# First feed-forward product by seven block products in both layers, the first 256 features plain, and background modulations in three tiles

## The chip, the cores and the metric

One Trainium2 chip, one of its cores. The metric is the device time of one execution in microseconds (us). Engine names in the profile: PE is TensorE's matrix multiply and PEld its weight load, DVE is VectorE, ACT is ScalarE, POOL is GpSimd, SP is SyncE, which issues all the DMAs here.

## What is computed

Two layers of a diffusion backbone run over 256 context tokens and 1024 latent tokens of width 1024. Each layer has a mixer (attention, a gated linear recurrence, a gated MLP) and then a feed-forward part, which alone is changed. `mod` is one vector of six modulations for each stream, computed from a conditioning vector.

```python
mod = silu(cond) @ w_ada[l] + b_ada[l]             # sh1, sc1, g1, sh2, sc2, g2
x   = layernorm(ALPHA * x + g1 * out, ln1_g, ln1_b)
hff = x * (1 + sc2) + sh2
f   = square(relu(hff @ w_ff1[l] + b_ff1[l])) @ w_ff2[l] + b_ff2[l]   # 1024 -> 4096 -> 1024
x   = layernorm(ALPHA * x + g2 * f, ln2_g, ln2_b)
```

All data are float32. Every matrix operand is split into a rounded high part and a low remainder, and each product is the sum of three: high by high, high by low, low by high.

## The kernel before

**Blocks and chunks.** Tokens come in ten blocks of 128: two of the context (group C, 256 columns) and eight of the latents (groups A and B, 512 columns each). The product with `w_ff1` has its output features on the partitions. It runs in 16 chunks (`NCH`) of 256 features, each chunk as two halves `m` of 128.

**The plain form** (`ff1`, layer 0) does for each half and group eight steps of the inner dimension, each with three matmuls (`fm_group`, `mm3`): 96 matmuls of 512 columns and 48 of 256 in a chunk. The weights of a chunk are two pieces, each split by ScalarE (high part, L168) and GpSimd (low part, L172, 128x1024) in `p_emit_split`. ScalarE takes the result out of PSUM with bias and ReLU.

**The seven-product form** (`first_seven`, layer 1, `SL = (1,)`) takes features, inner dimension and latents in two halves each and forms the latents' part of a chunk with seven block products instead of eight. A product has 12 matmuls of 512 columns; the context's columns stay plain, 48 matmuls of 256 columns. It needs sums and differences of weight blocks and of token blocks. For each chunk GpSimd forms four weight blocks (L1560 to L1565) and splits eight (`w1s`, L172), each operation 128x512; `wait` issues these items `WLA` = 4 products ahead. The seven results are combined by VectorE with seven additions that have one operand in PSUM (L1588). The token blocks' sums and differences (`half`, `hitem`) are made once, at the end of `out_proj` and between the products of chunk 0.

**What runs beside it.** `mid_store` writes each chunk's squared result to DRAM; for the first 12 chunks (`2*NQ`) VectorE adds and subtracts four times on 128x640 (L1476 to L1479). `residual` takes one block of the residual stream in each of eleven calls from chunk 2 on: a DMA load, two VectorE operations on 128x1024 (L1422, L1423), a DMA store. In layer 0, from chunk 1 on, a background generator (`ada_bg`) computes seven parts of the modulations, each in two halves of 512 columns. A half loads four slabs `aslab` of 512 KB, accumulates 16 times on VectorE (2 times L484, 14 times L486, 128x512), splits the sum (ScalarE, then GpSimd on 128x1024, `aspl`) and ends with four matmuls `ada` (L495). `tick(us)` advances it by `us * 0.62` (`ABR`) units, and each accumulation costs 0.6 units:

```python
nc.vector.scalar_tensor_tensor(acc[:, s, :], sl, self.sc[:, k, s:s + 1], acc[:, s, :], ALU.mult, ALU.add)
yield 0.6
```

**Order and buffers.** The framework orders each engine's instructions and places the waits; an engine runs its instructions in that order. Tiles of 4 KB a partition come from two pools, `u` (30 tiles) and, during a layer's feed-forward part, `x` (`NX` = 14 tiles), with 8 tiles `m` beside it. PSUM has 8 banks, shared by all products of the stage.

Of the kernel before, what the change touches and what calls it, by code (L numbers as in the profile page):

```python
# [15 lines left out]
P = 128  # L16
# [5 lines left out]
NCH = 16  # L22
# [19 lines left out]
SL = (1,)  # L42
WLA = 4
# [35 lines left out]
class Kern:  # L79
# [149 lines left out]
    def pieces_init(self):  # L229
# [8 lines left out]
        for l in range(DEPTH):  # L238
# [18 lines left out]
    def pal(self, p, stg=False):  # L257
# [5 lines left out]
        if ph == "out" and self.phase == "out" and not stg:  # L263
            return self.mt
        return self.x if ph == self.phase and self.X is not None else self.u
# [203 lines left out]
    def ada_bg(self, l, parts):  # L469
# [3 lines left out]
        for part in parts:  # L473
            for h in range(2):
                acc = self.u([P, 2, 512], s="aacc")
                c0 = part * D + h * 512
                for k in range(8):
                    if k % 2 == 0:
                        sl2 = self.u([P, 2, 512], s="aslab")
# [8 lines left out]
                hi, lo = (self.u([P, 2, 512], F32R, s="aspl") for _ in range(2))  # L488
# [8 lines left out]
                row = self.u([2, 2, 512], s="arow")  # L497
# [49 lines left out]
    def h_from_pair(self, h, t0, xa, xb, ab, lo_pool=None, alloc=None, tmp_act=False):  # L547
# [27 lines left out]

    def h_raw(self, h, t0, xa, xb, ab):

        nc = self.nc
        g = grp(t0)
        if g not in h:  # L580
            h[g] = [self.u([P, 2, 512], s="hr") for _ in range(4)]
        c0 = (t0 - GROUPS[g][0]) * P
        for kp in range(4):
            b = self.ps([P, 2, 256], "hps")
            for kk in range(2):
                k = 2 * kp + kk
                for j, x in enumerate((xa, xb)):
                    nc.tensor.transpose(b[:, kk, j * P:(j + 1) * P], x[:, k * P:(k + 1) * P], self.ident)
            for kk in range(2):
                k = 2 * kp + kk  # L590
                dst = h[g][kp][:, kk, c0:c0 + 256]
                if kk == 0:
                    nc.scalar.activation(dst, b[:, kk, :], AF.Identity, bias=ab[:, 1, 1, k:k + 1], scale=ab[:, 1, 0, k:k + 1])
                else:
                    nc.vector.tensor_scalar(dst, b[:, kk, :], ab[:, 1, 0, k:k + 1], ab[:, 1, 1, k:k + 1], ALU.mult, ALU.add)


    def run(self):
# [8 lines left out]
        for l in range(DEPTH):  # L607
# [12 lines left out]
            h2 = self.out_proj(l, mix)  # L620
            h1 = self.ff(l, h2)
            self.x_close()

    def cst_load(self):
# [32 lines left out]
        self.rows = self.DR.tile([2, D], F32, name="rows")  # L657
        self.ydr = [self.DR.tile([10, P, 4, P], F32, name=f"ydr{l}") for l in range(DEPTH)]
# [664 lines left out]
    def out_proj(self, l, mix):  # L1323
# [31 lines left out]
        for i, t in enumerate(BLOCKS):  # L1355
# [4 lines left out]
            if fs and i == len(BLOCKS) - 2:  # L1360
                fs["half"](0)
            if fs and i == len(BLOCKS) - 1:
                fs["half"](1)
                fs["h"](1)
# [9 lines left out]
            if i >= OW:  # L1374
                if fs:
                    fs["w"](i - OW + 1)
                else:
                    self.p_emit_split(min(self.pidx[(l, "w1", 0, 0)] + i - OW + 1, self.pidx[(l, "w1", 0, 1)] + 1))
            if fs and i == len(BLOCKS) - 1:
                del w  # L1380
# [14 lines left out]
            if len(xq) == 4 or (len(xq) == 3 and xq[0][0] % 2 == 0):  # L1395
                (ta, xa), (tb, xb) = xq.pop(0), xq.pop(0)
                if fs:
                    self.h_raw(h2, ta, xa, xb, ab)
                else:
                    self.h_from_pair(h2, ta, xa, xb, ab, lo_pool=None, tmp_act=True)  # L1400
# [3 lines left out]
        if fs:  # L1404
            fs["h"](2)
            h2["C"] = tuple([al([P, 4, 256], F32R, s="hc") for _ in range(2)] for al in (self.u, self.mt))
        self.late = lambda: self.h_from_pair(h2, ta, xa, xb, ab, lo_pool=None, tmp_act=bool(fs))
        return fs or h2


    def residual(self, l, alloc):
# [4 lines left out]

        def step(i):
            if i == 0:
                st["g"], st["b"] = (self.bc_row(I[k][l:l + 1], "a" + k[-1], ALPHA, alloc=alloc) for k in ("ln1_g", "ln1_b"))
# [16 lines left out]
    def ff1(self, l, c, h2, after):  # L1436
# [6 lines left out]
        for g in "ABC":  # L1443
# [3 lines left out]
            if g == "B":  # L1447
                self.ahead((l, "w1", c, 1), 2, 4, (l, "w1", NCH - 1, 1))
# [571 lines left out]
```

## Time and profile before

| | us |
|---|---|
| median of the runs (3178.54 to 3184.3) | 3180.42 |
| the profiled execution | 3182.43 |
| span from its first to its last instruction | 3180.6 |
| layer 0: first product, 16 chunks (741.40 to 1208.97) | 467.57 |
| layer 1: first product, 16 chunks (2288.62 to 2723.16) | 434.54 |

Times inside the program count from the span's start. The two last lines are read from the first matmul of the stage to the first of the next (tile `mh`, the second feed-forward product). PE is busy 94% of the span, DVE 72%, POOL 48%, ACT 46%.

### The profile page before, as it was taken

The numbers are of one execution on the slowest core, as the hardware profiler recorded it, in microseconds if no ns is written. First come the engines' busy times: TensorE is split into PE (matmuls) and PEld (weight loads), VectorE is DVE, ScalarE is ACT, GpSimd is POOL, SyncE is SP. The second block draws the span as 40 slices with busy tenths as digits, with TensorE's granted clock in tenths as the row PEclk, the third lists the DMA queues.
The fourth block names the chain that finished last, engine by engine and source line by source line (L and its number), as shares of the span: only waits on it lengthen the run. The fifth ranks groups of instructions, "written<-read, shape, count | busy, mean of one in ns | idle before, by whom it ended". The sixth has DMA issues, their size and how long they took to land. (4 is left out here: it accounts for less than half of the span.)

```text
span 3180.6 us, 42699 instructions
## 1 busy us (share of the span) xinstructions
PE 2978.2 (94%) x15816; PEld 2491.2 (78%) x15816; DVE 2281.1 (72%) x4540; ACT 1471.5 (46%) x2268; POOL 1527.9 (48%) x866
## 2 busy tenths in 40 slices
PE   6888999899999999999989889999889999999993
PEld 4677789788888888888777868997778888878883
DVE  8779999765666634878764989996744542487889
ACT  5554578744332324333166438884254444433301
POOL 3222244503322326856743213357565666685776
PEclk9999999999999999999999999999999999999997
DMA  7321000225666654443321110004235453544331
GB/s 226 117 90 56 15 1 8 74 96 191 219 216 228 206 188 148 157 138 112 116 100 34 53 31 1 1 25 138 96 112 174 168 176 137 191 147 145 114 109 66
DMA packets 163392, 367.44 MB, mean 116 GB/s; under 512 B 20792, under 2 KB 58440, under 8 KB 163184
## 3 DMA queue, kind: packets, MB, share of 16 engines
q1 hardware_dynamic: 163184, 364.72, 34.2%
q8 instruction: 124, 2.03, 0.3%
q14 instruction: 84, 0.69, 0.1%
HBM read 261.84 MB, written 102.83 MB: 115 GB/s over the span
## 5 line engine op out<-in xcount | busy, mean ns | idle before, releaser
L172 POOL TENSOR_TENSOR wlo<-stg,whi 128x1024 fp32r<-128x1024 f32 (+2 forms) x116 | 241.5, 2093 | 363.9 <-ACT whi L168 331.9
L176 PE MATMUL ps<-hh,whi 128*128 128x512 f32 (+1 forms) x1040 | 376.7, 363 | 14.3 <-ACT htmp L570 12.4
L177 PE MATMUL ps<-hl,whi 128*128 128x512 f32 (+1 forms) x1040 | 374.4, 360 | 4.5 <-POOL hl L390 2.6
L178 PE MATMUL ps<-hh,wlo 128*128 128x512 f32 (+1 forms) x1040 | 373.5, 359 | 0.0
L176 PE MATMUL ps<-wh,mh 128*128 128x512 f32 x840 | 333.1, 397 | 0.7 <-DVE accy L1770 0.7
L177 PE MATMUL ps<-wl,mh 128*128 128x512 f32 x840 | 331.8, 395 | 0.0
L178 PE MATMUL ps<-wh,ml 128*128 128x512 f32 x840 | 330.7, 394 | 0.0
L172 POOL TENSOR_TENSOR pt<-ptf,pt 128x512 fp32r<-128x512 f32 x128 | 166.6, 1302 | 241.8 <-DVE pt L170 225.8
L172 DVE TENSOR_TENSOR ml<-mf,mh 128x1280 fp32r<-128x1280 f32 x84 | 173.7, 2067 | 118.1 <-ACT mh L168 112.5
L1179 DVE TENSOR_SCALAR_CACHE_REDUCE S<-sc 128x512 f32<-128x512 f32 (+1 forms) x416 | 224.8, 582 | 14.7 <-PE pT L1190 12.5
L168 ACT CAST mh<-mf 128x1280 fp32r<-128x1280 f32 x84 | 106.3, 1265 | 278.8 <-PE ps L177 235.6
L176 PEld LDWEIGHTS ps<-hh,whi 128*128 128x128 f32 x1040 | 196.5, 189 | 47.4 <-ACT htmp L570 12.8
L172 POOL TENSOR_TENSOR wl<-wraw,wh 128x1024 fp32r<-128x1024 f32 x60 | 170.6, 2851 | 117.0 <-ACT wh L168 116.9
L177 PEld LDWEIGHTS ps<-hl,whi 128*128 128x128 f32 x1040 | 196.9, 189 | 37.9 <-POOL hl L390 4.4
L178 PEld LDWEIGHTS ps<-hh,wlo 128*128 128x128 f32 x1040 | 197.6, 190 | 32.8 <-issue 0.2
L1182 ACT ACTIVATE S<-S,anm 128x1280 f32<-128x1280 f32 (+1 forms) x160 | 191.2, 1196 | 38.4 <-DVE anm L1181 36.1
L1190 PE MATMUL pT<-ident,S 128*128 128x128 f32 x1344 | 202.6, 274 | 2.0 <-DVE pt L1199 1.4
L1215 PE MATMUL o<-pt,vt 128*128 128x256 f32 x1024 | 193.1, 304 | 9.7 <-POOL pt L172 7.9
L177 PE MATMUL ps<-slo,w1s 128*128 128x512 f32 x448 | 180.4, 403 | 16.3 <-DVE slo L1504 16.2
L1588 DVE TENSOR_TENSOR f<-ps,f 128x512 f32<-128x512 f32 x112 | 75.8, 688 | 163.2 <-PE ps L178 152.8
L176 PEld LDWEIGHTS ps<-wh,mh 128*128 128x128 f32 x840 | 157.7, 188 | 39.5 <-DVE accy L1770 1.5
L178 PEld LDWEIGHTS ps<-wh,ml 128*128 128x128 f32 x840 | 157.7, 188 | 39.2
(394 smaller groups left out, 8550.0 us busy)
## 6 DMA issues: line engine op xcount, KB each, us to landing
mf<-mc SPq DMA_DIRECT2D x84, 640.0 KB
mc<-s SPq DMA_DIRECT2D x48, 640.0 KB
aslab<-in_w_ada SPq DMA_DIRECT2D x56, 512.0 KB
stg<-in_w_ff SPq DMA_DIRECT2D x48, 512.0 KB
wraw<-in_w_ff SPq DMA_DIRECT2D x48, 512.0 KB
mc<-f SPq DMA_DIRECT2D x72, 320.0 KB
w1r<-in_w_ff SPq DMA_DIRECT2D x32, 512.0 KB
stg<-in_w_in SPq DMA_DIRECT2D x28, 512.0 KB
```

The source lines that it names most:

```text
L168: nc.scalar.copy(hi, src)
L172: e.tensor_tensor(lo, src, hi.bitcast(F32), ALU.subtract)
L176: mm(out, lh, rh, start=start, stop=False)
L177: mm(out, lh, rl, start=False, stop=False)
L178: mm(out, ll, rh, start=False, stop=stop)
L1179: nc.vector.tensor_scalar(S[:, c0:c0 + n], b[:, :n], 1.0, -3.0e38, ALU.mult, ALU.max, accum_out=u["m"][:, hh, i:i + 1])
L1182: nc.scalar.activation(S[:, :c0], S[:, :c0], AF.Exp, bias=u["nm"][:, hh:hh + 1], accum_out=u["d"]["den"][:, ci % 2, hh:hh + 1])
L1190: nc.tensor.transpose(b[:, c, hh, :], u["S"][hh][:, (2 * j + c) * P:(2 * j + c + 1) * P], self.ident)
L1215: nc.tensor.matmul(o, v, pt[:, hl, c, :], start=j == 0 and c == 0 and hl == 0, stop=j == last and c == 1 and hl == 1)
L1588: add = lambda x, b, y: nc.vector.tensor_tensor(x, b, y, ALU.add)
```

## The change

Both layers take the seven-product form from chunk 1 on (`SL = (0, 1)`, `C0 = 1`); chunk 0 is plain in both. `out_proj` therefore forms the split token blocks with `h_from_pair` in layer 1 too, as layer 0 did, and in both layers also stores the unsplit values to a DRAM tensor `hr`. During chunk 0 they are loaded back (eight tiles of 512 KB) and the sums and differences are formed and split; three of the seven token operands are the plain chunk's own tiles. The context blocks' late transposes move to the middle of chunk 0's group B. `WLA` goes from 4 to 3, and a chunk's weights are loaded at item 6 of the chunk before instead of item 0. `ada_bg` takes its tiles from `x` and lets go of a slab before the next is taken. `tick` is called after each product and each context half. `residual` works on two blocks by half their columns instead of one whole block; the count and size of its operations stay.

```diff
-SL = (1,)
-WLA = 4
+SL = (0, 1)
+C0 = 1
+WLA = 3
@@ pieces_init
-            for c in range(NCH if l not in SL else 0):
+            for c in range(C0 if l in SL else NCH):
@@ ada_bg
-                acc = self.u([P, 2, 512], s="aacc")
+                acc = self.x([P, 2, 512], s="aacc")
-                        sl2 = self.u([P, 2, 512], s="aslab")
+                        sl = sl2 = None
+                        sl2 = self.x([P, 2, 512], s="aslab")
...
+                sl = sl2 = None
+                hi, lo = (self.x([P, 2, 512], F32R, s="aspl") for _ in range(2))
@@ h_from_pair
+            if raw is not None and kp % 2:
+                nc.sync.dma_start(out=raw["AB".index(g), kp // 2, :, :, c0:c0 + 256], in_=tmp2.rearrange("p a k n -> p (a k) n"))
@@ out_proj
-                if fs:
-                    self.h_raw(h2, ta, xa, xb, ab)
-                else:
-                    self.h_from_pair(h2, ta, xa, xb, ab, lo_pool=None, tmp_act=True)
+                self.h_from_pair(h2, ta, xa, xb, ab, lo_pool=None, tmp_act=True, raw=self.hr[l] if fs else None)
@@ ff1
             for m in range(2):
+                if l in SL and g == "B" and m:
+                    self.run_late()
@@ first_seven
+        def hload(g, hf, alloc):
+            t = [alloc([P, 2, 512], s="hr") for _ in range(2)]
+            for i in range(2):
+                nc.sync.dma_start(out=t[i], in_=self.hr[l][g, hf, :, 2 * i:2 * i + 2, :])
+            return t
+        def hstep(at):
+            if at == (0, 0):
+                H[0], H[1], H[5] = ((h[g][0][i:i + 2], h[g][1][i:i + 2]) for g, i in (("A", 0), ("A", 2), ("B", 2)))
+                hr["raw"] = [hload(g, hf, self.x if (g, hf) == (0, 1) else self.u) for g, hf in ((1, 1), (1, 0), (0, 0), (0, 1))]
+            elif at == (0, 1):
+                a22, a21, a11, a12 = hr.pop("raw")
+                s1 = hr["s1"] = a22
+                comb(nc.vector, s1, a21, a22, ALU.add)
+                hr["s2"], hr["s3"] = a11, a21
+                comb(nc.vector, a21, a11, a21, ALU.subtract)
+                comb(nc.vector, a11, s1, a11, ALU.subtract)
+                s4 = hr["s4"] = a12
+                comb(nc.gpsimd, s4, s4, hr["s2"], ALU.subtract)
+                hsplit(2, hr.pop("s2"))
+                hsplit(3, hr.pop("s3"))
+            elif at == (C0 - 1, 2):
+                hsplit(4, hr.pop("s1"))
+                hsplit(6, hr.pop("s4"))
...
             if j == 0:
-                if c == 0:
-                    load(0)
+                if c == C0:
+                    load(c)
+            if j == 6:
                 load(c + 1)
...
+                self.tick(2.8)
@@ ff
             def after(g):
+                if fs and c < C0:
+                    if c == 0 and g == "A":
+                        fs["wait"](8 * C0 + 4)
+                    fs["h"]((c, "ABC".index(g)))
...
-            if l in SL:
-                h2["run"](c, prep)
+            if fs and c >= C0:
+                fs["run"](c, last_chunk)
```

`halloc`, `half` and `hitem` go. `comb` is two operations on 128x1024; `hsplit` makes for each of two tiles a ScalarE copy and a VectorE subtraction on 128x1024.

## Rows read from the trace of the kernel before

**Rows 1.** The page, busy time: engine, us, share of the span, instructions.

```profile
span 3180.6 us, 42699 instructions
PE 2978.2 (94%) x15816; PEld 2491.2 (78%) x15816; DVE 2281.1 (72%) x4540; ACT 1471.5 (46%) x2268; POOL 1527.9 (48%) x866
```

**Rows 2.** Windows over layer 0's product, layer 1's chunks 0 and 1, its chunks 2 to 15.

```profile
core 0: us, PE busy (x) PEld busy (x) DVE busy (x) ACT busy (x) POOL busy (x), PEclk, DMA share, GB/s
741.40:1208.97 467.57, 465.13 (x2377) 386.75 (x2376) 279.21 (x363) 152.37 (x192) 137.28 (x49) 1.00 0.60 205
2288.62:2369.05 80.43, 61.97 (x282) 48.71 (x280) 50.40 (x77) 44.54 (x76) 50.67 (x37) 0.87 0.22 73
2369.05:2723.16 354.11, 354.11 (x1851) 300.42 (x1850) 151.08 (x163) 157.66 (x236) 218.30 (x163) 1.00 0.50 174
```

**Rows 3.** Timeline of PE in layer 0's product: start, duration, engine, line, tiles.

```profile
741.40 0.40 PE L176 MATMUL ps<-hh,whi 128*128 128x512 f32 x1
...
763.18 1.91 PE L560 MATMUL hps<-ident,r 128*128 128x128 f32 x16
767.04 0.74 PE L176 MATMUL ps<-hh,whi 128*128 128x256 f32 x3 [1.96 <-ACT hh L568]
...
906.51 0.40 PE L178 MATMUL ps<-hh,wlo 128*128 128x512 f32 x1
906.75 0.39 PE L495 MATMUL ada<-aspl,sel 128*2 128x512 f32 x1
...
935.84 0.39 PE L495 MATMUL ada<-aspl,sel 128*2 128x512 f32 x1
```

**Rows 4.** Timeline of PE in layer 1: the starts of chunks 3 and 4.

```profile
2394.34 0.40 PE L176 MATMUL ps<-shi,w1s 128*128 128x512 f32 x1
...
2419.64 0.40 PE L176 MATMUL ps<-shi,w1s 128*128 128x512 f32 x1
```

**Rows 5.** Windows inside layer 1's chunk 0, columns as in rows 2.

```profile
2299.80:2311.00 11.20, 4.87 (x16) 3.54 (x15) 10.49 (x20) 4.53 (x8) 6.29 (x5) 0.70 0.47 142
2311.00:2322.00 11.00, 6.84 (x28) 4.05 (x26) 9.62 (x9) 10.33 (x22) 9.23 (x6) 0.84 0.01 3
2322.00:2333.00 11.00, 8.54 (x25) 6.62 (x26) 6.02 (x14) 7.39 (x15) 8.01 (x6) 0.69 0.01 1
```

**Rows 6.** Groups by line, layer 0, 876.8 to 1047: count, busy, mean ns, idle before.

```profile
L486 DVE SCALAR_TENSOR_TENSOR aacc<-aslab,scond,aacc 128x512 f32<-128x512 f32 x84 | 64.1, 817 | 10.2 <-DMA aslab<-in_w_ada 10.2
L484 DVE TENSOR_SCALAR aacc<-aslab,scond 128x512 f32<-128x512 f32 x12 | 5.3, 474 | 11.5 <-DMA aslab<-in_w_ada 11.5
```

**Rows 7.** Groups of POOL by line, layer 1, 2400 to 2600.

```profile
L172 POOL TENSOR_TENSOR w1s<-w1r,w1s 128x512 fp32r<-128x512 f32 x47 | 64.8, 1385 | 41.7 <-ACT w1s L168 41.6
L172 POOL TENSOR_TENSOR w1s<-w1t,w1s 128x512 fp32r<-128x512 f32 x16 | 20.7, 1296 | 34.3 <-ACT w1s L168 34.3
L1563 POOL TENSOR_TENSOR w1r<-w1r 128x512 f32<-128x512 f32 x8 | 10.4, 1301 | 0.0
```

**Rows 8.** Timeline of layer 0, GpSimd and VectorE (other engines' rows left out).

```profile
975.59 6.23 POOL L172 TENSOR_TENSOR wlo<-stg,whi 128x1024 fp32r<-128x1024 f32 x1 [11.37 <-ACT whi L168]
...
975.69 2.72 DVE L486 SCALAR_TENSOR_TENSOR aacc<-aslab,scond,aacc 128x512 f32<-128x512 f32 x4
...
978.34 1.21 DVE L1423 TENSOR_TENSOR rn<-rn,ab 128x1024 f32<-128x1024 f32 x1
...
981.78 2.41 POOL L172 TENSOR_TENSOR aspl<-aacc,aspl 128x1024 fp32r<-128x1024 f32 x1
```

**Rows 9.** Timeline of layer 1, GpSimd and VectorE (other engines' rows left out).

```profile
2398.57 3.13 POOL L172 TENSOR_TENSOR w1s<-w1r,w1s 128x512 fp32r<-128x512 f32 x2
...
2399.34 1.21 DVE L1476 TENSOR_TENSOR s<-f,f 128x640 f32<-128x640 f32 x1 [5.38 <-ACT f L1638]
...
2400.47 1.91 DVE L1478 TENSOR_TENSOR s<-f 128x640 f32<-128x640 f32 x1
...
2402.30 0.81 DVE L1477 TENSOR_TENSOR s<-s,f 128x640 f32<-128x640 f32 x1
```

**Rows 10.** One line's instructions, 2345 to 2720: count, duration ns min/median/max.

```profile
L1588 DVE TENSOR_TENSOR f<-ps,f x104: 678/691/694, 2349.9 to 2717.7; 128x512 f32<-128x512 f32 x104
```

More of the change, by code (lines that the diff above doesn't have):

```diff
@@ L264, in pal @@
             return self.mt
+        if key[1] == "w1" and key[0] in SL and self.X is not None:
+            return self.x
         return self.x if ph == self.phase and self.X is not None else self.u
@@ L657, in cst_load @@
         self.rows = self.DR.tile([2, D], F32, name="rows")
+        self.hr = {l: self.DR.tile([2, 2, P, 4, 512], F32, name=f"hr{l}") for l in SL}
         self.ydr = [self.DR.tile([10, P, 4, P], F32, name=f"ydr{l}") for l in range(DEPTH)]
@@ L1374, in out_proj @@
             if i >= OW:
-                if fs:
[L1376 to L1380, printed above, removed]
+                self.p_emit_split(min(self.pidx[(l, "w1", 0, 0)] + i - OW + 1, self.pidx[(l, "w1", 0, 1)] + 1))
             r = self.x(s="r")
@@ L1490, in first_seven @@
         raw, T, W, H = {}, {}, {}, {}
-        done = [0]
+        done = [8 * C0]
         tt = nc.gpsimd.tensor_tensor
-        def halloc(key):
-            H[key] = tuple([self.u([P, 2, 512], F32R, s=n) for _ in range(2)] for n in ("shi", "slo"))
-        def hsplit(key, src):
-            halloc(key)
-            e = nc.gpsimd if key == 5 else nc.vector
-            for i in range(2):
-                for k in range(2):
-                    hi, lo, x = H[key][0][i][:, k], H[key][1][i][:, k], src[i][:, k]
-                    nc.scalar.copy(hi, x)
-                    self.keep(e.tensor_tensor(lo, x, hi.bitcast(F32), ALU.subtract))
@@ L1506, in first_seven @@
-        hr = {}
-        def half(j):
-            if j == 0:
-                A, B = h["A"], h["B"]
-                hr.update(a11=A[0:2], a12=A[2:4], a21=B[0:2], a22=B[2:4])
-                halloc(0)
-                hr["s1"] = [self.u([P, 2, 512], s="hs1") for _ in range(2)]
-            else:
-                h.pop("A"), h.pop("B")
-            c = lambda k, i: hr[k][i][:, :, j * 256:j * 256 + 256]
-            for i in range(2):
-                tt(c("s1", i), c("a21", i), c("a22", i), ALU.add)
-            for i in range(2):
-                hi, lo = (H[0][e][i][:, :, j * 256:j * 256 + 256] for e in range(2))
-                nc.scalar.copy(hi, c("a11", i))
-                self.keep(nc.vector.tensor_tensor(lo, c("a11", i), hi.bitcast(F32), ALU.subtract))
-            for i in range(2):
-                self.keep(nc.vector.tensor_tensor(c("a21", i), c("a11", i), c("a21", i), ALU.subtract))
-            for i in range(2):
-                self.keep(nc.vector.tensor_tensor(c("a11", i), c("s1", i), c("a11", i), ALU.subtract))
@@ L1529, in hitem @@
[L1529 to L1540 removed]
+        hr = {}
@@ new lines, in hload @@
+        def hload(g, hf, alloc):
[3 more added lines that the diff above has]
+            return t
+        def hsplit(key, src):
+            H[key] = ([], [])
+            while src:
+                x = src.pop(0)
+                for k, n in enumerate(("shi", "slo")):
+                    H[key][k].append(self.u([P, 2, 512], F32R, s=n))
+                self.split(H[key][0][-1], H[key][1][-1], x, lo_eng="dve")
+                del x
@@ L1641, in run @@
                 h.pop("C")
-        return dict(h=hitem, half=half, w=wait, run=run)
+        return dict(h=hstep, wait=wait, run=run)
     def mid_load(self, l, c, alloc):
```

107 lines of the change are left out of this document (38 added, 69 removed).

## Prediction

> **What bounds the kernel now.** I read the page first: TensorE is busy 94% of the span [rows 1], so only stages in which it computes more than it must, or waits, have anything to give. Then the windows over the two first products [rows 2]. Layer 0's plain chunks hold TensorE for 465 of 467.57 us. Layer 1's chunks 2 to 15 hold it for all of 354.11 us, but its chunks 0 and 1 take 80.43 us with TensorE busy for 62. The timeline gives the price of a chunk. Plain: 29.09 us from one `ada` group to the next (935.84 - 906.75), of which the group's four matmuls are four steps of 0.24, so 28.15 without it [rows 3]. Seven products: 2419.64 - 2394.34 = 25.30 us [rows 4]. So TensorE bounds both steady states, and the start of layer 1's product is bound by preparing its operands.
>
> The next view is the one that I think decides: the timelines of GpSimd and VectorE side by side. In rows 8 GpSimd's subtraction starts at 975.59 while VectorE runs six operations in a row, and ends at 981.82, 2.27 us after VectorE's last (978.34 + 1.21 = 979.55); the next one, with VectorE idle, takes 2.41. In rows 9 GpSimd's second operation ends at 2401.70, 1.15 us after VectorE's first (2400.55), and VectorE's second ends 0.68 us after that, though it had started at 2400.47 and its neighbour takes 0.81. So two elementwise operations that read SBUF on these two engines take turns. VectorE's additions out of PSUM do not: 104 of them, with GpSimd busy 62% of the time around them (218.30 of 354.11, rows 2), all last 678 to 694 ns [rows 10].
>
> **The change, as TensorE sees it.** Layer 0: chunk 0 becomes 28.15 + 1.91 for the late transposes [rows 3] = 30.1, and 15 chunks take 25.30, with 14 `ada` groups of 0.94 beside them: 30.1 + 379.5 + 13.2 = 422.8, against 467.57: 44.8 less. Layer 1: 80.43 - 25.30 = 55.1 for chunk 0 now becomes 30.1: 25.0 less. Together 69.8 less, if nothing else binds. The context's wait at 767.04 (1.96 us, rows 3) goes as well, since the transposes move ahead of it; it lies inside the 467.57.
>
> **The change, as the turns see it.** I add what the two engines must do by turns in one chunk of layer 0, chunks 2 to 11:
> - GpSimd forms four weight blocks and splits eight, 12 operations on 128x512. Alone they take 1.30 [rows 7], after a VectorE operation 1.15 [rows 9]; I take 1.20 (most would now follow one): 14.4. Today's two splits of 128x1024 a chunk go.
> - The background: 9 ticks of 2.8 at 0.62 are 15.6 units a chunk. A half costs 13.3 units (a gate) or 16.3, mean 15.0 over the 14, so 1.04 halves a chunk: 14.6 of L486, 2.1 of L484 and 1.04 splits. L486 in a row takes 0.66 (four in 2.72, rows 8); with 0.13 off 0.74, as for the 0.68 above, 0.61; I take 0.62: 9.1. L484 is 0.47 by its mean [rows 6]; I take 0.40 in a row: 0.8. Split 2.27 [rows 8]: 2.4.
> - The residual: two of 128x1024, 1.21 alone [rows 8], 1.1 by turns: 2.2. Its half columns and pairs leave count and size as they were.
> - `mid_store`: four of 128x640, 0.81 and 0.68 [rows 9], 0.7: 2.8.
>
> Sum 31.7 us a chunk, where TensorE needs 25.30 + 0.97 = 26.3. Before, GpSimd's weight work in a chunk was two operations, and the turns fitted well inside 29.09. Ends: all by the short readings (1.15, 0.61, no L484, 0.68) 29.8; all by the full durations 35.4. I take 31.7, nearest to rows 8 and 9, and add 4% for turns left empty between ScalarE's copy and GpSimd, a choice that no row gives: 33.0 us.
>
> The Trainium skill (SBUF — State Buffer, Who interferes with whom) says that a VectorE instruction with two SBUF inputs and a GpSimd one that reads SBUF exclude each other for the whole instruction, the second fully blocked, and that an operand in PSUM is spared. Rows 8 to 10 agree, but the blocked one ends 0.13 us sooner than its full duration; by the rule's letter the sum would be the 35.4 of the high end, by the rows 31.7. It also says that a tensor-scalar operation with one SBUF input can exclude GpSimd; no row here has L484 against a GpSimd operation, and without it the sum would be 30.9.
>
> Layer 0 in full. Group A of chunk 0 is 48 steps of 0.235, 11.2 us. From its end to the end of chunk 1 the turns hold: the new sums and splits of token blocks (14 VectorE operations of 128x1024 at 1.1 and two GpSimd ones at 2.27: 19.9), 19 weight operations (22.8: seven in advance for chunk 1), two `mid_store` (5.6), the background (12.3), the late context subtractions (eight of 128x256, a quarter of 1.21 each: 2.4): 63; some weight work comes before group A ends, so 60, where TensorE needs 45. Chunks 0 and 1: 71. Chunks 2 to 11: 330. Chunk 12 has no `mid_store`, 30.1; chunk 13 no residual, 27.8. In chunk 14 the background runs out (14 / 1.04 = 13.5 chunks) and TensorE binds again, 26; chunk 15, 25.3. Sum 510, 43 more than 467.57.
>
> Layer 1 has no background: 14.4 + 2.2 + 2.8 = 19.4 of 25.30, so TensorE stays the bound, with three products (8.4 us) of weights in advance instead of four, against a `mid_store` and residual burst of 5. Its start, without the 12.3, is 51 of turns against 44, and needs eight tiles of 512 KB back from DRAM: at the 205 GB/s of layer 0's product [rows 2] the 4.2 MB take 20 us from the end of group A, as long as groups B and C of chunk 0 last. I take 5 us of stall; ends 0 and 15. So 25.0 - 5 = 20 less.
>
> **Edits costed at nothing.** Storing `hr` (16 DMAs of 512 KB over `out_proj`) is hidden while that stage keeps TensorE busy and a temporary tile waits for its store; uncovered it would be a few us a layer. A slab let go before the next is taken costs nothing while another of `x`'s 14 tiles is free; in rows 6 VectorE already idles 10.2 + 11.5 us in six chunks for slabs. Bytes a chunk stay (the same weights, slabs, stores), so the DMA share of 0.60 [rows 2] rises only as the chunk shortens. Loading weights at item 6 leaves some five products, 14 us, for 1 MB: hidden, but a late load now stops GpSimd, then TensorE. In `out_proj` of layer 1 the splitting replaces the sums that `half` made there, work of like size on the same engines.
>
> Sum: the profiled execution's 3182.43 + 43 - 20 = 3205; it lies 2.0 above the median of the runs, so 3203 for the median.
>
> **The rivals.** Let P be the time of one turn-bound chunk of layer 0; its part that scales with P is 13.6 chunks long (71 - 11.2, ten chunks, two shorter ones, over 33.0). The sign turns where layer 0 loses what layer 1 gains: 467.57 + 20 = 11.2 + 51.3 + 13.6 P, P = 31.3.
> - *The turns run short* (P about 30, the low end, nothing left empty): layer 0 comes out even, 62.5 + 408 = 470, and layer 1's start is what is left: 3158 to 3180. For it: my sum before the 4% is 31.7, close to the turn. Against: nothing is then ever empty. Chance 0.17.
> - *TensorE stays the bound everywhere*, the turns being hidden in GpSimd's idle time, which the windows show: 38% in layer 1 [rows 2]. Then 3180.4 - 69.8 = 3111, up to 3135 with starts of 12 us. Against it are rows 8 and 9. Chance 0.13.
> - *Stalls cost clock too.* In layer 1's start TensorE was busy 44 to 78% with a granted clock of 0.69 to 0.84 [rows 5], between its two levels of 1.2 and 2.4 GHz, and 1.00 in the steady stretches [rows 2]. At P = 33 it is busy 26.3 / 33 = 80%. If it then gets 0.69, as at 78% in rows 5, a chunk is 26.3 / 0.69 = 38 us: layer 0 579, total 3272. Slabs that wait for a tile would act alike. Chance 0.13.
>
> **How the numbers follow.** My forecast, P of 31.5 to 36, has 0.52: 3203, its own range 3185 to 3245. No change, where layer 0's loss happens to meet layer 1's gain, takes 0.05. The range is 3140 to 3270: it leaves out the hidden case and the upper half of the clock case. 0.2% (6.4 us) is about what a measurement of this kernel tells from no change. Faster: 0.13 + 0.15 of the short turns = 0.28. Same: 0.05 and the rest of the short turns, 0.07. Slower: 0.65.
>
> **What the profile after would show.** Right: in layer 0 chunks of about 33 us in the middle, GpSimd's `w1s` well above 1.30 and L486 well above 0.74 in the mean there, TensorE idle behind GpSimd's `w1s`, and 25.3 us again from chunk 14 on; in layer 1 chunks of 25.3 us and a chunk 0 of 30 to 35. Wrong: chunks of 26.3 us in layer 0 with TensorE full (the turns did not bind), or chunks of 38 at a lowered clock. A wait of VectorE for slabs as the main idle time in layer 0 would say that the tiles, not the turns, were the bound.

## The result, and the profile after

The changed kernel takes 3228.86 us in the median of four runs (3226.97 to 3232.43), the kernel before, beside it, 3182.36 (3178.54 to 3185.44): a ratio of 1.0149, 95% interval 1.0134 to 1.0163. It is slower by 46.5 us where 23 were forecast. The sign and the range held; the size did not. The profiled execution is the longest of the four (3232.43 us), 3.6 us above their median, so the windows below add up to somewhat more than the 46.5.

The page's busy times, which answer to [rows 1]: VectorE and GpSimd rise, TensorE falls, and the span is 50.1 us longer.

```profile
span 3230.7 us, 43148 instructions
PE 2968.9 (92%) x15648; PEld 2476.9 (77%) x15648; DVE 2422.1 (75%) x4640; ACT 1536.0 (48%) x2410; POOL 1713.9 (53%) x1002
```

Windows over the stages, columns as in [rows 2]: all of layer 0's first product, then its chunks 0 and 1, chunks 2 to 11, chunk 12 and chunk 14; layer 1's chunks 0 and 1, the second half of its chunk 0, and its chunks 2 to 15.

```profile
core 0: us, PE busy (x) PEld busy (x) DVE busy (x) ACT busy (x) POOL busy (x), PEclk, DMA share, GB/s
737.70:1277.70 540.00, 456.47 (x2198) 369.34 (x2198) 419.54 (x466) 201.45 (x303) 329.99 (x201) 0.90 0.55 184
...
737.70:806.40 68.70, 61.87 (x296) 51.71 (x296) 55.26 (x69) 32.77 (x51) 30.47 (x19) 0.90 0.53 177
806.40:1154.40 348.00, 285.39 (x1364) 228.34 (x1363) 289.06 (x312) 121.71 (x182) 214.87 (x131) 0.89 0.58 191
1154.40:1191.10 36.70, 28.93 (x138) 23.17 (x138) 28.33 (x29) 11.96 (x18) 25.67 (x17) 0.86 0.53 171
...
1218.30:1252.40 34.10, 28.62 (x138) 22.93 (x138) 19.20 (x21) 14.37 (x23) 28.35 (x21) 0.90 0.25 87
...
2351.00:2418.10 67.10, 58.33 (x293) 49.21 (x292) 42.21 (x55) 32.81 (x52) 35.28 (x24) 0.92 0.47 160
...
2371.00:2392.00 21.00, 12.23 (x60) 10.54 (x59) 16.57 (x16) 10.31 (x19) 7.01 (x3) 0.76 0.32 106
...
2418.10:2773.20 355.10, 355.10 (x1851) 301.43 (x1850) 145.87 (x163) 162.50 (x243) 231.70 (x166) 1.00 0.50 176
```

Layer 0's first product takes 540.0 us where it took 467.57 [rows 2]. Its ten middle chunks take 34.8 us each, with TensorE idle for 62.6 of 348 us; before, TensorE was full there. Layer 1's takes 422.2 (67.1 + 355.1) where it took 434.5. So the span's +50.1 is +72.4 in layer 0's first product, -12.3 in layer 1's, -8.9 in the stretch from the last four chunks of layer 0's second product (tile `midh`) to layer 1's input projections (234.6 us for 243.5, by the first matmuls of the stages; below it is called the stretch behind the second product), -3.7 ahead of layer 0's product, and 2.6 in small pieces.

Groups by line and form in layer 0's middle chunks, 806.5 to 1154.3, answering to [rows 6, 7 and 10]. The lines of the code have moved: L490 was L486, L488 was L484, L1569 was L1588, L500 was L495.

```profile
L500 PE MATMUL ada<-aspl,sel 128*2 128x512 f32 x40 | 18.7, 565 | 62.2 <-ACT aspl L169 51.5 <-POOL aspl L173 10.6
...
L490 DVE SCALAR_TENSOR_TENSOR aacc<-aslab,scond,aacc 128x512 f32<-128x512 f32 x143 | 144.9, 1065 | 1.2 <-DMA aslab<-in_w_ada 1.1
L1569 DVE TENSOR_TENSOR f<-ps,f 128x512 f32<-128x512 f32 x70 | 47.0, 684 | 38.3 <-PE ps L179 37.8
...
L488 DVE TENSOR_SCALAR aacc<-aslab,scond 128x512 f32<-128x512 f32 x20 | 15.4, 812 | 0.3 <-POOL w1t L1541 0.3
...
L173 POOL TENSOR_TENSOR w1s<-w1r,w1s 128x512 fp32r<-128x512 f32 x60 | 88.8, 1498 | 45.7 <-ACT w1s L169 45.7
L173 POOL TENSOR_TENSOR w1s<-w1t,w1s 128x512 fp32r<-128x512 f32 x20 | 40.4, 2022 | 8.9 <-ACT w1s L169 8.9
L173 POOL TENSOR_TENSOR aspl<-aacc,aspl 128x1024 fp32r<-128x1024 f32 x10 | 25.1, 2514 | 77.7 <-ACT aspl L169 69.1 <-PE ps L179 8.5
```

Operations that read SBUF on both engines have grown in the mean (L490 from 817 ns, `w1s` from the 1296 and 1385 of layer 1 before), the additions out of PSUM (L1569) have not. That is the mark of turns. But TensorE does not stand behind `w1s`, as forecast; nearly all its idle time, 62.2 us, is ahead of the modulations' matmuls, and these wait for ScalarE's copy of a sum that VectorE is late with. VectorE in turn stands 37.8 us for TensorE's products, and GpSimd 69.1 for the same copy.

The timeline of VectorE, ScalarE, GpSimd and TensorE through one such place, and below it the start of layer 1 (rows left out between):

```profile
1024.91 3.79 DVE L490 SCALAR_TENSOR_TENSOR aacc<-aslab,scond,aacc 128x512 f32<-128x512 f32 x4
...
1025.57 1.26 POOL L173 TENSOR_TENSOR w1s<-w1r,w1s 128x512 fp32r<-128x512 f32 x1 [5.59 <-ACT w1s L169]
...
1029.32 2.74 DVE L490 SCALAR_TENSOR_TENSOR aacc<-aslab,scond,aacc 128x512 f32<-128x512 f32 x4
...
1032.14 1.04 ACT L169 CAST aspl<-aacc 128x1024 fp32r<-128x1024 f32 x1 [6.66 <-DVE aacc L490]
...
1033.24 0.58 PE L500 MATMUL ada<-aspl,sel 128*2 128x512 f32 x1 [7.44 <-ACT aspl L169]
...
1033.27 2.37 POOL L173 TENSOR_TENSOR aspl<-aacc,aspl 128x1024 fp32r<-128x1024 f32 x1 [6.44 <-ACT aspl L169]
...
1033.62 0.63 PE L177 MATMUL ps<-shi,w1s 128*128 128x512 f32 x1
...
1039.23 0.39 PE L179 MATMUL ps<-shi,w1s 128*128 128x512 f32 x1
...
1039.66 1.29 DVE L1569 TENSOR_TENSOR f<-ps,f 128x512 f32<-128x512 f32 x2 [7.00 <-PE ps L179]
...
2372.78 1.23 DVE L1499 TENSOR_TENSOR hr<-hr,hr 128x1024 f32<-128x1024 f32 x1 [6.68 <-DMA hr<-hr]
2375.01 6.90 DVE L1499 TENSOR_TENSOR hr<-hr,hr 128x1024 f32<-128x1024 f32 x4 [1.00 <-DMA hr<-hr]
2381.83 6.00 DVE L579 TENSOR_TENSOR hc<-htmp,hc 128x256 fp32r<-128x256 f32 x8
...
2382.30 0.58 PE L178 MATMUL ps<-hc,whi 128*128 128x256 f32 x1 [6.88 <-DVE hc L579]
```

First TensorE waits 7.44 us while VectorE makes the last sums; then VectorE waits 7.00 us for TensorE's next product, and GpSimd, which had stood 6.44 us in its order behind the same copy, runs alone. The engines take turns not only for SBUF but in waiting for each other, so that the turns that both need are at times used by neither. A stall costs clock too: matmuls that follow each other by 0.23 us at 1039 do so by 0.43 after the wait.

In layer 1 the loads of `hr` come late (6.68 and 1.00 us, and once more before), VectorE's sums of them stand ahead of the context's subtractions, and TensorE waits 6.88 us for these.

### The profile page after: what moved, and what is told of

The parts are those of the page before. It is cut to its first block, busy times and chain, and to the rows that moved or that the text cites. A ratio compares the mean times of both kernels' runs of the same rounds, so it can differ in the third digit from the quotient of the medians.

```text
span 3230.7 us, 43148 instructions
## 1 busy us (share of the span) xinstructions
PE 2968.9 (92%) x15648; PEld 2476.9 (77%) x15648; DVE 2422.1 (75%) x4640; ACT 1536.0 (48%) x2410; POOL 1713.9 (53%) x1002
## 5 line engine op out<-in xcount | busy, mean ns | idle before, releaser
L173 POOL TENSOR_TENSOR w1s<-w1r,w1s 128x512 fp32r<-128x512 f32 x180 | 249.4, 1402 | 145.2 <-ACT w1s L169 145.2
L1569 DVE TENSOR_TENSOR f<-ps,f 128x512 f32<-128x512 f32 x210 | 141.0, 686 | 198.0 <-PE ps L179 188.1
L173 POOL TENSOR_TENSOR wlo<-stg,whi 128x1024 fp32r<-128x1024 f32 (+2 forms) x88 | 156.2, 1791 | 197.8 <-ACT whi L169 179.7
L1568 ACT ACTIVATE f<-f,pfm 128x512 f32<-128x512 f32 x120 | 86.3, 721 | 257.7 <-DVE f L1569 256.9
L490 DVE SCALAR_TENSOR_TENSOR aacc<-aslab,scond,aacc 128x512 f32<-128x512 f32 x196 | 197.1, 1058 | 5.7 <-DMA aslab<-in_w_ada 5.7
L177 PE MATMUL ps<-shi,w1s 128*128 128x512 f32 x480 | 196.0, 408 | 0.0
L179 PE MATMUL ps<-shi,w1s 128*128 128x512 f32 x480 | 193.4, 403 | 0.5 <-POOL w1s L173 0.5
L178 PE MATMUL ps<-slo,w1s 128*128 128x512 f32 x480 | 193.3, 403 | 0.0
L178 PEld LDWEIGHTS ps<-wl,mh 128*128 128x128 f32 x840 | 157.7, 188 | 38.5
```

The costliest lines, as they stand in the source:

```text
L173: e.tensor_tensor(lo, src, hi.bitcast(F32), ALU.subtract)
L177: mm(out, lh, rh, start=start, stop=False)
L178: mm(out, lh, rl, start=False, stop=False)
L179: mm(out, ll, rh, start=False, stop=stop)
L1568: relu = lambda x, y, m: nc.scalar.activation(x, y, AF.Relu, bias=bias[m])
L1569: add = lambda x, b, y: nc.vector.tensor_tensor(x, b, y, ALU.add)
```

## The experiments

Stages are compared by their length, from the first matmul of the one to the first of the next: it is less disturbed than the total, since the stretch behind the second product takes 233 to 245 us in kernels that have the same code there. "L0" and "L1" are the first product's lengths in the two layers: 467.6 and 434.6 before, 540.0 and 422.2 after. Where no interval is given, the time is one run; four runs of the changed kernel lie 5.5 us apart.

**Layer 1 alone.** The change with layer 0 left plain.

```diff
-SL = (0, 1)
+SL = (1,)
```

> Layer 0 plain in all 16 chunks, layer 1 as in the change (chunk 0 plain). If layer 0's loss comes from its seven products and layer 1 gains by itself, layer 0 is back at 468 us, layer 1 keeps its 20 us gain, and the time is 3158 to 3166, below the kernel before. If instead the common edits (WLA 3, late weight loads, residual by halves, slabs let go) cost layer 0, it stays above 475 and the time above 3170.

3177.22 us, ratio 0.9996 (0.9987 to 1.0005). L1 is 423.7, as in the full change, so all of the loss is layer 0's. But L0 is 478.6, 11 us longer than before, from edits that both forms share; the expectation missed by that.

**The same with the modulations' tiles as before.** Tiles from `u`, slabs overlapping.

```diff
-                acc = self.x([P, 2, 512], s="aacc")
+                acc = self.u([P, 2, 512], s="aacc")
...
-                        sl = sl2 = None
-                        sl2 = self.x([P, 2, 512], s="aslab")
+                        sl2 = self.u([P, 2, 512], s="aslab")
```

> Seven products in layer 1 alone, as before (3177.22 us, layer 0's first product 478.6 against 467.6 in the kernel before), but with the modulations' tiles taken from the other pool and their slabs overlapping, as in the kernel before. If these two edits cost layer 0 its 11 us, it takes 466 to 470 again and the total is 3164 to 3169. If the rest did it (the raw stores, the context's place, the weights' pool), layer 0 stays at 475 to 480 and the total at 3174 to 3180.

3172.49 us, ratio 0.9979 (0.9969 to 0.9988), L0 472.4: between the two bands. The tiles cost 6 of the 11 us; the other 5 are in none of these edits. TensorE there still waits 2.7 us for GpSimd's part of the split sums, which it did not before; what made the rest is open.

**No wait for the sums.** The modulations' matmuls read a token tile of chunk 0 (`cw`) instead of the split sums, so that the modulations are not those of the reference; all else runs.

```diff
-                        nc.tensor.matmul(b[0:2, :], self.sel[:, s, :], w[:, s, :], start=s == 0 and w is hi, stop=s == 1 and w is lo)
+                        nc.tensor.matmul(b[0:2, :], self.sel[:, s, :], self.cw, start=s == 0 and w is hi, stop=s == 1 and w is lo)
```

> The four ada matmuls of each half read a ready block of the latents instead of the split sum, so TensorE never waits for the background (the modulations are not the reference's); all work of VectorE, GpSimd and ScalarE stays. Theory A: turns delay the accumulation, TensorE's queue stands at the ada matmuls behind it (62 us in ten chunks), and these waits leave turns empty: chunks 2 to 11 fall from 34.8 to 31.5 to 32.5 us and the total to 3185 to 3200. Theory B: the turns hold 34.8 by themselves, the wait merely shows up at ada: TensorE then waits as long for w1s, the chunks stay at 34 to 35 and the total at 3220 to 3230. Theory C, tiles and DMA of the slabs: no change either.

3218.18 us; L0 520.0, yet chunks 2 to 11 still take 34.8 us; chunks 0, 1 and 14 are what got shorter. TensorE's three groups with most idle time ahead of them, 806.5 to 1154.3 (six groups on weight blocks have 56.2 us together, `ada` has none):

```profile
L177 PE MATMUL ps<-shi,w1s 128*128 128x512 f32 x163 | 67.9, 416 | 12.5 <-ACT w1s L169 12.5
...
L179 PE MATMUL ps<-hh,w1s 128*128 128x512 f32 x120 | 51.4, 428 | 12.6 <-POOL w1s L173 12.6
L177 PE MATMUL ps<-hh,w1s 128*128 128x512 f32 x120 | 51.3, 427 | 12.1 <-ACT w1s L169 12.1
```

The wait has moved from the sums to the weight blocks. So the `ada` wait is only where the shortage shows in these chunks: the preparation of operands as a whole is too slow.

**More and less by turns.** Two more GpSimd operations a chunk (two that are made twice), and, in another kernel, the weight blocks' low parts on VectorE (0.68 us for 1.15 on GpSimd).

```diff
-                tt(t[:, 0], r1[:, 0], r0[:, 0], ALU.subtract)
-                tt(t[:, 1], r1[:, 1], t[:, 0], ALU.subtract)
+                for _ in range(2):
+                    tt(t[:, 0], r1[:, 0], r0[:, 0], ALU.subtract)
+                for _ in range(2):
+                    tt(t[:, 1], r1[:, 1], t[:, 0], ALU.subtract)
```

> In each chunk of both layers GpSimd's two operations that form w1t are issued twice (same result): 12 operations become 14. By turns, layer 0 gets 2 x 1.15 to 1.3 longer in some 13 chunks, 25 to 35 us, and layer 1 nothing, since its 19.4 plus 2.4 is still under 25.3: total 3254 to 3264. If GpSimd has room in layer 0 (it is busy 60 to 70% there, waits included) and something else holds the chunks, below 8 us in all.

```diff
-            self.split(w[:, 0], w[:, 1], src)
+            self.split(w[:, 0], w[:, 1], src, lo_eng="dve")
```

> The changed kernel with the eight low parts of a chunk's weight blocks subtracted by VectorE instead of GpSimd. A subtraction of 128x512 is 1.15 us of turns on GpSimd and about 0.6 on VectorE, so the turns of a layer 0 chunk fall by 4.4 us of 31.7 while VectorE gets 5 us more work. By the turns, chunks 2 to 11 fall from 34.8 to 29 to 31 and the total by 45 to 70 us, to 3160 to 3185. If VectorE's own queue is what is full (28 of 34.8 us busy, waits included) and the turns are only a part of it, the chunks get longer by up to 5 us: 3240 to 3300. Layer 1 stays at 25.3 a chunk by both.

3258.77 us, L0 563.2: 23.2 longer (a little under the 25 to 35 of the expectation), or about 1.9 in each middle chunk for two operations of some 1.2. And 3182.62 us, L0 491.7: 48.3 shorter, although VectorE, the busiest of the preparing engines, got eight operations a chunk more. The sum of both engines' work by turns went down. GpSimd's own work did too, but GpSimd is idle for 133 of the 348 us of the changed kernel's middle chunks, so its own work is not what fills them.

**More for VectorE out of turn.** Two of the additions that have an operand in PSUM are made twice in each chunk.

```diff
-            add(q[0, 0], prod(1), q[1, 0])
+            b = prod(1)
+            for _ in range(2):
+                add(q[0, 0], b, q[1, 0])
```

(the same for product 3)

> The changed kernel with two of the seven additions out of PSUM issued twice in every chunk from 1 on (same result): 1.37 us more work for VectorE in a chunk, none of it by turns. By the turns alone, GpSimd uses that time and layer 0 gets 0 to 8 us longer. If VectorE's queue is the bound, 1.37 x 13.6 = 19 us longer, total 3247. Layer 1 nothing by both.

3239.53 us, L0 546.1. 1.37 us more of VectorE a chunk cost 0.4 in the mean of the 15 chunks (6.1 together), and 0.65 in the ten middle ones. The stage is within the 0 to 8 of the first theory, the total, 10.7 longer, between the two. VectorE's own work counts, but for less than work by turns (0.65 for 1.37, against 1.9 for 2.4).

**The sums in PSUM.** The same VectorE operations, the accumulator in two PSUM banks; the sum is split in two halves, the low part by VectorE.

```diff
-                acc = self.x([P, 2, 512], s="aacc")
+                acc = [self.ps(s="aacc") for _ in range(2)]
...
-                            nc.vector.scalar_tensor_tensor(acc[:, s, :], sl, self.sc[:, k, s:s + 1], acc[:, s, :], ALU.mult, ALU.add)
+                            nc.vector.scalar_tensor_tensor(acc[s], sl, self.sc[:, k, s:s + 1], acc[s], ALU.mult, ALU.add)
...
-                self.split(hi, lo, acc)
+                for s in range(2):
+                    self.split(hi[:, s, :], lo[:, s, :], acc[s], lo_eng="dve")
```

> The background accumulates in two PSUM banks, so its VectorE operations have one operand in SBUF, and the low part of its sum is taken by VectorE out of PSUM: 9 us of accumulation and 2.4 of splits a chunk leave the turns; VectorE's own work stays about 23 us a chunk, DMA and slabs stay, products have six banks left. Theories A and B: turns fall to 20 us, TensorE binds at 26.3 a chunk, layer 0 takes 425 to 440 instead of 536, total 3118 to 3135, below the kernel before by 50 us or more. Theory C, slabs and tiles: chunks stay above 33 and the total above 3200. If VectorE in its order is the bound, about 30 a chunk and 3175.

3149.75 us, ratio 0.9903 (0.9886 to 0.9919): faster than both kernels, 79 us below the changed one, though short of what was expected. L0 is 452.2. The window of that stage and VectorE's accumulations in its middle chunks:

```profile
738.30:1190.50 452.20, 430.64 (x2197) 355.18 (x2196) 366.49 (x494) 204.72 (x319) 266.48 (x188) 0.98 0.65 220
```

```profile
L490 DVE SCALAR_TENSOR_TENSOR aacc<-aslab,scond,aacc 128x512 f32<-128x512 f32 x154 | 106.1, 744 | 3.1 <-DMA aslab<-in_w_ada 3.1
```

L490 takes 744 ns in the mean for 1065, with GpSimd busy for 59% of the stage (266.48 of 452.20) against 61%. Over the whole stage none of its 196 instructions lasts longer than 757 ns, though 95 of them overlap one of GpSimd; in the changed kernel 65 of 196 last over 800, up to 1835. The Trainium skill (SBUF — State Buffer, Who interferes with whom) says that a VectorE operation with at most one SBUF input, outside its two-port modes, does not contend with GpSimd; the 757 ns at most agree. The stage got 88 us shorter without an operation less on VectorE. Not all of that need be the operand's: the edit also moves the sums' subtraction to VectorE (worth 3.3 us alone, in the last experiment) and gives `x` a tile back, which no run has alone.

**The same, the matmuls later.** A half's matmuls come after the third step of the next half's sums, and its split parts stay that long in `x`; otherwise as the version above.

```diff
+                    if k == 2 and pend is not None:
+                        yield from self.ada_end(l, *pend)
+                        pend = None
```

> The background in PSUM, as in the run before it, and each half's four ada matmuls, with what follows them, issued after the sixth accumulation of the next half instead of right behind the split. The run with PSUM alone took 452 us in layer 0's product against TensorE's own 423, with 17.5 us in ten chunks in front of ada. If that order is what is left, layer 0 takes 425 to 435 and the total 3125 to 3137. If VectorE, busy 89% there, is what holds the chunks, the wait moves to the products and the total stays at 3145 to 3152.

3187.95 us, ratio 1.0035 (1.0021 to 1.0049), L0 488.1, 36 us longer. In its middle chunks (800 to 1150) TensorE waits for weight blocks again and VectorE for slabs:

```profile
L177 PE MATMUL psc<-hc,w1s 128*128 128x256 f32 x176 | 55.5, 315 | 23.6 <-ACT w1s L169 23.6
...
L491 DVE SCALAR_TENSOR_TENSOR aacc<-aslab,scond,aacc 128x512 f32<-128x512 f32 x160 | 110.9, 746 | 11.4 <-DMA aslab<-in_w_ada 11.3
```

L491 keeps its 746 ns, so turns are not what came back. That `x`'s tiles, held longer, are missing for weights and slabs is the reading that fits both waits; no run with more tiles was made.

**Sums of token blocks in written order.** On top of the edit above, `comb` keeps its place, so that the context's subtractions are not behind it.

```diff
-                e.tensor_tensor(dst[i], a[i], b[i], op)
+                self.keep(e.tensor_tensor(dst[i], a[i], b[i], op))
```

> As the run before it, and the sums of token blocks on VectorE and GpSimd are held behind everything issued before them, so that the late context blocks are ready when group C of chunk 0 wants them. In the changed kernel layer 1's chunk 0 waits 8.8 us for that low part, of the 12.6 us by which layer 1's product (422.2) is over TensorE's 409.6. If the order on VectorE is the cause, each layer gains 4 to 9 us: 8 to 18 less than the run before it. If the turns of the start hold it anyway, the wait goes to the products that need the sums and the total is within 4 us of the run before it.

3182.25 us, ratio 1.0014 (1.0004 to 1.0024); L1 is 425.7 for 422.6. TensorE's wait at layer 1's start moved from `hc` to the split of the sums (`slo`, 7.8 us): whichever comes second is late. VectorE no longer waits for the loads there; it stands idle for 9.86 us, in its order, ahead of the context's subtractions (for ScalarE's `htmp`), and the sums start behind these. The total is 5.7 us below the edit above, between the two bands, but by the stretch behind the second product and not by the first products, of which both got longer (L0 490.4).

**The first product of each sum on ScalarE.** On top of the sums in PSUM.

```diff
-                            nc.vector.tensor_scalar(acc[s], sl, self.sc[:, k, s:s + 1], None, ALU.mult)
+                            nc.scalar.mul(acc[s], sl, self.sc[:, k, s:s + 1])
```

> The version with the modulations' sums in PSUM (3149.75 us, first product of layer 0 452.2), with the first of the eight products of each sum (k = 0) now made by ScalarE, which has no turn with GpSimd in the traces so far. Turns: these k = 0 operations have one SBUF input and took turns in the changed kernel (812 ns mean against 479); some 2.1 of them a chunk leave VectorE, 1 to 1.7 us. If VectorE, busy 250 of 280 us in the middle chunks, still sets the pace there, layer 0's first product loses 4 to 15 us more: 437 to 448, total 3135 to 3147. If TensorE binds those chunks already (26.3 us is its own time), nothing: 3147 to 3152. If ScalarE, which splits the sums and copies the weight blocks first, becomes late by it: longer than 3152.

3132.97 us, ratio 0.9852 (0.9836 to 0.9869), the fastest kernel here; below its band. L0 is 445.1, 7.1 less and in the band; another 7 come from the stretch behind layer 0's second product, which took 233.0 for 240.2 with the same code. TensorE is idle for 15 of 445 us:

```profile
736.60:1181.70 445.10, 430.23 (x2198) 356.51 (x2197) 341.96 (x466) 223.24 (x349) 267.28 (x189) 0.98 0.66 226
```

**How far ahead the weights are made.** `WLA` is 3 in the change. Two, four and five in the changed kernel, and four in the fastest version.

```diff
-WLA = 3
+WLA = 2
```

> The changed kernel (3228.86 us, first product of layer 0 540.0, chunks 2 to 11 34.8 us in the mean) with weights prepared two products ahead instead of three. If the empty 12% of the turns in the middle chunks comes from the short lead of the preparation (ScalarE's copy, GpSimd's subtraction and TensorE's use following each other closely), a shorter lead empties more: chunks 36 to 38 us, total 3245 to 3275. If the engines' queue orders leave the turns empty whatever the lead, chunks stay at 34 to 35.5 and the total at 3222 to 3238.

> The changed kernel (3228.86 us, first product of layer 0 540.0) with weights prepared four products ahead instead of three. Two ahead gave 3253.37 and 563.1, so 23 us hung on that one product of lead. If the lead still is short at three (the short lead explains the empty turns), four ahead gives back a good part of it: first product of layer 0 515 to 530, total 3205 to 3220. If three is enough and what is left is the turns' own work and the wait of the modulations' matmuls for their sums, which a longer lead does not shorten: 535 to 545, total 3223 to 3234. In neither case does it fall to the 3180 of the kernel before.

> The changed kernel with weights five products ahead. If the lead explains the empty turns: shorter than four ahead by up to another 10 us. If not, or if the blocks held longer take x's tiles from the slabs and the residual (as when the halves were held longer, 3187.95 against 3149.75): 3228 to 3250.

> The fastest version (sums in PSUM, their k = 0 products on ScalarE, 3132.97 us; first product of layer 0 445.1) with weights four products ahead. Its middle chunks mostly stand at TensorE's own 26.3 us; what is left over 26.3 a chunk is 445 - 423 = 22, nearly all in chunks 0 to 2 and one of 29.5. A longer lead gives 0 to 8 of it: 3125 to 3133. If the further blocks take x's tiles from the token blocks and slabs, it is slower: 3135 to 3150.

| products ahead | total | L0 | L1 |
|---|---|---|---|
| 2 | 3253.37 | 563.1 | 423.4 |
| 3 (the change) | 3228.86 | 540.0 | 422.2 |
| 4, ratio 1.024 (1.022 to 1.026) | 3255.09 | 536.5 | 446.2 |
| 5 | 3268.34 | 555.9 | 437.7 |
| fastest version, 3 | 3132.97 | 445.1 | 423.7 |
| fastest version, 4, ratio 0.999 (0.998 to 0.9999) | 3177.29 | 451.4 | 448.6 |

A lead of two is too short, as expected. Four gives L0 the 535 to 545 of the second theory, so a longer lead, with the same 14 tiles, does not fill the empty turns. The total missed, since L1 lost 24 us, which neither theory had: VectorE there waits 47.8 us for the residual's loads (`rn`), and TensorE 14.7 us for ScalarE (`f`). That a fourth block in `x` leaves these loads no tile in time is argued from the 14 tiles, not shown. Five products ahead and the fastest version with four lie above every band that was given for them (3250 and 3150).

**The place of the sums' subtraction.** GpSimd stood 69 to 78 us in its order ahead of it. In one kernel it is issued 2.8 units later, at nearly the same cost of a half in units (12.8 for 12.6 up to the matmuls), for which the sums' steps come 0.5 units apart instead of 0.6; in the other VectorE makes it.

```diff
-                        yield 0.6
+                        yield 0.5
...
+                nc.scalar.copy(hi, acc)
+                yield 2.8
...
+                nc.gpsimd.tensor_tensor(lo, acc, hi.bitcast(F32), ALU.subtract)
...
-                yield 3.0
+                yield 2.0
```

> The changed kernel (3228.86 us, first product of layer 0 540.0) with the subtraction of each modulations' half put 2.8 units of pace later behind ScalarE's copy; the paces of the half's other steps are shortened, so that a half costs the same. Work by turns is unchanged. In the changed kernel GpSimd stood idle 78 of 348 us before that subtraction, for a copy that waits for VectorE's sums, while weight operations stood behind it in GpSimd's order. If this place in the order leaves the turns empty (12% where 4% was forecast), GpSimd's idle time there mostly goes, chunks 2 to 11 fall from 34.8 to 31 to 33 us, the stage to 500 to 525, and the total to 3188 to 3214. If the turns' amount of work alone sets the pace, the idle time goes elsewhere, and the stage stays at 530 to 545, the total at 3219 to 3234.

```diff
-                self.split(hi, lo, acc)
+                self.split(hi, lo, acc, lo_eng="dve")
```

> The changed kernel with the subtraction of each modulations' half on VectorE instead of GpSimd, in place. It frees GpSimd's order as the run beside it, and takes about 1.1 us out of the turns for each half (1.21 for 2.27 in the kernel before), at VectorE's cost. If the order is what leaves turns empty: first product of layer 0 490 to 515, total 3178 to 3204. If the amount of work by turns alone counts: by the slope of the two runs that changed it (0.75 us of chunk for 1 us of turns) 0.8 us a chunk, stage 527 to 533, total 3216 to 3222.

Later: 3220.46 us, L0 523.5, chunks 2 to 11 33.8 us. On VectorE: 3225.15, L0 536.7. GpSimd's groups in the second kernel, 806.5 to 1154.3, and TensorE's in the first:

```profile
L173 POOL TENSOR_TENSOR w1s<-w1r,w1s 128x512 fp32r<-128x512 f32 x61 | 98.8, 1634 | 146.6 <-ACT w1s L169 146.2 <-DVE arow L508 0.4
```

```profile
L503 PE MATMUL ada<-aspl,sel 128*2 128x512 f32 x40 | 18.1, 548 | 45.5 <-ACT aspl L494 36.2 <-POOL aspl L497 9.3
```

With the subtraction gone from GpSimd, its idle time is found ahead of `w1s` instead, and the stage gains 3.3 us, less than either theory gave: GpSimd's order is not the cause. Issuing it later also moves TensorE's matmuls later and the sums closer together; the matmuls' wait falls from 62.2 to 45.5 us, and the stage by 16.4. That splits the theories: the stage is in the band of the first (500 to 525), its chunks are above theirs (31 to 33), and the total is in the band of the second (3219 to 3234), as the first twelve chunks of the second product took 5.7 us longer (300.5 for 294.8). Which of the moves gave the 16.4 us no run tells.

## Why the prediction was right, and why its size was not

*That the turns bind layer 0* was right. Work by turns added or taken moves the stage (+23.2, -48.3), the edit that puts one operand in PSUM takes 88 us from it at the same count of VectorE's accumulations, and with the `ada` wait gone the middle chunks stay as long.

*The sum of 31.7 us a chunk* was near. In the trace after, the operations with two operands in SBUF and GpSimd's, each counted back from its end for the shortest duration of its group and overlaps counted once, fill 0.87 of chunks 2 to 11: 30.4 of 34.8 us. With the multiplications L488, which the forecast's sum held, it is 0.89, or 31.1 us. This is an estimate from durations; the trace does not record the turns themselves.

*The 4% for empty turns, "a choice that no row gives", is the step that failed.* By the same count 11 to 13% are empty, 3.7 to 4.4 us of a chunk where 1.3 was forecast. With a sum that was a little high, that makes 34.8 for 33.0 us a chunk, or 18.0 us over the ten. The count of 0.87 becomes 0.82 with two products ahead; in the fastest version, whose accumulations have only one operand in SBUF and do not count, it is 0.73, and TensorE is the bound there. What makes the turns empty is partly shown: issuing the subtraction and matmuls later, with the sums closer together, made it 0.91 used and took 1 us from a chunk. GpSimd's order is ruled out, and a longer lead within the same tiles did not help. The rest stays open; by the timeline the engines, each bound to its order, wait for each other around the end of each half, but no run took that apart.

*The chunks at the end* failed with it: chunk 12 was 36.7 for 30.1 and chunk 14 34.1 for 26. They were priced as if what is left out of a chunk came off in full, and as if a background that runs out had no wait at its end; the last halves' matmuls came at 1208 and 1233 us, in chunks 13 and 14. Chunks 0 and 1 came out at 68.7 for 71, chunk 13 at 27.2 for 27.8, chunk 15 at 25.3. Together: -2.3 + 18.0 + 6.6 - 0.6 + 8.1 = 29.8, the 540 for 510.

*Layer 1's 5 us of stall* were 11.7: 67.1 less 30.1 and 25.3. The bounds of 0 and 15 held it, and the wait named, tiles coming back from DRAM, is the one in the timeline (11.7 us of VectorE's idle time there are `hr` loads), with the context's subtractions queued behind it. The other chunks take 25.36 for 25.30, 0.9 us more over 14. So 12.3 less instead of 20.

*Edits costed at nothing.* Slabs: right, 1.1 us of VectorE's waits in the middle chunks. Storing `hr`: right in layer 0, where the stage before the product takes 120.5 us for 120.4; 1.7 us in layer 1 (122.1 for 120.4). Three products ahead: right, and the best of the four leads tried by the total; two and four cost some 25 us more. The modulations' tiles: 6 us in a plain layer 0, where slabs were the only cost looked for. The 8.9 us gained behind layer 0's second product were not foreseen; since the same stretch takes 233 to 245 us over these kernels, nothing is built on them. With the 3.7 us gained ahead of layer 0's product they hid part of the miss: that the total is not 12.6 us further off is luck.

*Against the rivals.* Turns running short: no, 34.8 is above even the forecast's 33.0. TensorE as the bound: no, it is idle for 62.6 us. Stalls cost clock too: partly. In chunks 2 to 11 the granted clock is 0.89 in the mean, and TensorE is busy 285 us where ten chunks need 263; the rival had 0.69 and 38 us. How much of those 22 us would be lost at a full clock, with TensorE waiting anyway, no run tells.

*What the profile after was to show.* `w1s` and L490 grew as said and chunks 2 to 11 came within 2 us; but TensorE does not stand behind GpSimd's `w1s` (0.5 us), and 25.3 returns with chunk 15, not 14.

## What to carry to other kernels

Before work is moved to GpSimd beside a busy VectorE, add up, for one period, the operations of both that took turns here (VectorE's with two operands in SBUF, its multiplications into SBUF, GpSimd's weight operations) and compare the sum with TensorE's time; where in-order engines feed each other, do not count on all of a period: here the pair was in use for 87 to 89% (30.4 to 31.1 of 34.8 us) and TensorE already stood waiting; the best that a change of order reached was 0.91, by the count that gives 0.87. The way out was not a shorter wait or a longer lead but one operand in another memory: an accumulator in PSUM turned a change that cost 1.5% into one that gains 1.0%, and with its first product on ScalarE 1.5%. A longer lead was no way out either: four products instead of three cost 26 us in one kernel and 44 in another, more than half of it in layer 1.

## What was not expected of the hardware

- VectorE's multiplication with one SBUF input (L488) took 474 ns in the mean before [rows 6] and 812 beside the busier GpSimd: it takes turns too. The Trainium skill (SBUF — State Buffer, Who interferes with whom) says that tensor-scalar operations can enter a mode that contends with GpSimd; this agrees. The mean mixes two kinds: alone it takes some 480 ns, behind a GpSimd operation up to 1560. Writing to PSUM all 28 took 731 to 756 ns, 23 of them beside a GpSimd operation: the turns are gone, but the operation itself is longer. The two-input L490 gains a third by PSUM (744 for 1065) and pays nothing.
- After TensorE's wait of 7.44 us its matmuls of 512 columns last 0.63 us and follow each other by 0.43, for 5 us, and then by 0.23. The window over those 5 us shows the lower of the clock's two levels:

```profile
1033.20:1038.20 5.00, 4.80 (x11) 2.81 (x12) 0.00 (x0) 1.03 (x2) 4.84 (x3) 0.50 0.12 48
1038.20:1047.00 8.80, 8.80 (x47) 7.48 (x46) 6.41 (x10) 3.66 (x6) 2.13 (x2) 0.99 0.43 144
```
